# Second MLP of a two-layer hybrid step: the second product of blocks 0 to 2 by seven products of quarters, x kept in DRAM

## The chip, the cores and the metric

The kernel runs on one core of one Trainium2 chip. The metric is the device time of one execution in microseconds, taken as the median of three runs. Engines are named as in the profile: PE (TensorE matmul), PEld (TensorE weight load), DVE (VectorE), ACT (ScalarE), POOL (GpSimd), SP (SyncE, which here only issues DMAs).

## The reference: what is computed

One inference step of a trunk of two layers over 128 context tokens and 512 latent tokens, width 1024. Layer 0 mixes tokens by pooling, layer 1 by bidirectional retention; each layer then has an MLP of width 4096. Both sub-layers of a layer are gated by a per-channel vector that differs for context and latent tokens:

```
h = rmsnorm(x, norm_mlp_w[i]) * (1 + sc_m) + sh_m
x = x + g_m * (square(relu(h @ w1)) @ w2)
```

All inputs and outputs are f32. After the second MLP one more norm gives the outputs.

## The kernel before

All 640 tokens stay in SBUF transposed: `xall` is [128, 8, 640], eight slices of 128 channels; the tokens are handled in two halves of 320 (`HALF`, index h). Half 0 holds latent tokens alone. In half 1 the last 128 columns are context tokens with a gate of their own, so what is scaled by a gate there takes two instructions (192 and 128 columns, `PARTS`).

**Products.** f32 accuracy comes from operands that are split in a high and a low part (`split`, L142 to 146: ACT casts the high part, L144; DVE subtracts it from the source, L145). A product of two split operands is three matmuls (`mm3`, L205 to 207), each 128x128 weights times 128x320 activations. Weights come by SP as pieces of 1 MB (`load`), and are split when they are next needed.

**The MLP** (`mlp`, from L747) goes over four blocks of 1024 hidden channels. In each block the first product (w1) gives the hidden tiles, each passed through relu and square on ACT (L851, L852) and split into the operands `a` of the second product; the second product (w2) is `gemm`, eight output slices by two halves, 24 matmuls each, and DVE adds each result times the gate to x (`add_to_x`, L500).

In blocks 1 to 3 (`FAST`) the first product is made by **seven products of quarters** in place of eight: `quarters` (L767) makes sums and differences of the four quarters of h once (48 DVE instructions of 320 columns: L776 to 783 and the splits); `seven` (L790) makes the weight sums (L802 to 806, 128x1024 each) and splits; `fast` (L812) runs the seven products p = 0 to 6, 12 matmuls for each of two slices t, twice per block (half 0 and 1 of the block's channels), and combines the results on ACT and DVE (L832 to 842). In block 0 the first product is ordinary: slices 0 to 3 in `follow`, right behind the norm, slices 4 to 7 by `gemm`. Before, the instructions of `quarters` stand between those of block 0's second product.

**What sets the order.** Each engine runs its own list in order; the lists come from the order of the program text and a scheduler at build time, so an instruction waits behind all that stand ahead of it on its engine. Seven tiles `t` (`th()`, L131) serve as scratch for all of this. In the second MLP (the last stage of the kernel, before the last norm) i is 1.

Of the kernel before, what the change touches and what calls it, by code (L numbers as in the profile page):

```python
# [27 lines left out]
DV = 512  # L28
# [35 lines left out]

STEPS = (((0, 0, 0, 0, 3, 2, 3, 0), (0, 1, 0, 1, 0, 0, 0, 0)),
# [45 lines left out]
def hybrid_kernel(ctx: ExitStack, tc: tile.TileContext, x_prompt, x_sample, state_ret, c, c_ctx, w_ada, b_ada,  # L111
# [15 lines left out]
    tmp = ctx.enter_context(tc.tile_pool(name="tmp", bufs=1))  # L127
    psum = ctx.enter_context(tc.tile_pool(name="psum", bufs=8, space=PSUM))


    def bank():  # L131
        return psum.tile([128, 512], F32, tag="ps", name=nm("ps"))

# [4 lines left out]
    def t5():  # L138

        return tmp.tile([128, 512], F32, tag="t", name=nm("t"), bufs=7)  # L140
# [68 lines left out]
    def gemm(ws, act, h, mid=None):  # L209


        out = [bank()[:, 0:HALF] for _ in ws]
        for k in range(len(act)):
            if mid and k == len(act) // 2:
                mid()
            for o, w in zip(out, ws):
                mm3(o, [z[:, k] for z in w], [z[:, HALVES[h]] for z in act[k]], k == 0, k == len(act) - 1)
        return out
# [8 lines left out]
    tab_sb = const.tile([128, C_N], F32, name="tab_sb")  # L227
    nc.scalar.dma_start(out=tab_sb[:, 0:C_ROPE], in_=tab[:, 0:C_ROPE])
    ident = tab_sb[:, C_ID:C_ID + 128]
    ones_d = const.tile([128, 128], F32, name="ones_d")  # L230
    V.memset(ones_d, 1.0 / D)
    ones_v = const.tile([128, 128], F32, name="ones_v")
    V.memset(ones_v, 1.0 / DV)
# [184 lines left out]
    xall = xp.tile([128, KD, TOK], F32, name="xall")  # L418
# [132 lines left out]
    with tc.tile_pool(name="pool", bufs=1) as pp:  # L551
        extra[:] = [(wst, 2), (pp, 3), (pp, 3), (wst, 2), (pp, 3)]
# [89 lines left out]
        def load_tables():  # L642
            nc.sync.dma_start(out=win_sb, in_=win)
            nc.sync.dma_start(out=tab_sb[:, C_ROPE:], in_=tab[:, C_ROPE:])
# [61 lines left out]
    def decays():  # L706
# [25 lines left out]

        npos = const.tile([128, 896], I16, name="npos")
        G.iota(npos, [[1, 896]], base=-384, channel_multiplier=-1)
        ipos = const.tile([128, 2, 512], I16, name="ipos")
        G.iota(ipos[:, 0, :], [[1, 512]], base=1, channel_multiplier=0)
        G.iota(ipos[:, 1, :], [[-1, 512]], base=512, channel_multiplier=0)
# [7 lines left out]
        tables.extend((lg, nlg, npos, ipos, zeta))  # L745
# [3 lines left out]
    def mlp(i, sq, norm, hm, step, along):  # L749

        with tc.tile_pool(name=f"hid{i}", bufs=1) as hid:

# [7 lines left out]
            def get(b, n):  # L760

                for o in range(1, AHEAD + 1):
                    if b * 8 + n + o < 64 and not ((b * 8 + n + o) // 16 in FAST[i] and (b * 8 + n + o) // 8 % 2 == 0):
                        gets[(b * 8 + n + o) // 8]((n + o) % 8)
                return gets[b](n)
# [79 lines left out]

            for b in range(4):
                act = [[hid.tile([128, TOK], F32R, tag=f"a{n}{e}", name=nm("a")) for e in "hl"] for n in range(8)]

                def hidden(n, h, ps):
                    r, f = th(), th()  # L850
                    S.activation(r, ps, AF.Relu)  # L851
                    S.activation(f, r, AF.Square)  # L852
                    split(f, *[z[:, HALVES[h]] for z in act[n]])
# [9 lines left out]
                if b in FAST[i]:  # L863
                    if b == FAST[i][0]:
# [6 lines left out]
                    get(2 * b + 1, 0)  # L871
                else:
                    for n in range(4 if b == 0 else 0, 8):
                        if n == FREE:
                            room[0] = room[1]
                        for h in range(2):
                            hidden(n, h, gemm([get(2 * b, n)], hm, h)[0])
                        step(STEPS[b][0][n])
                if i == 0 and b == 0:
                    step(until=(0, 5))  # L880
                if b == 3:
                    room[:] = [None, None]
                    return tail(lambda n, h: gemm([get(7, n)], act, h)[0], mod[i][5], along)
                for n in range(KD):
# [22 lines left out]
    with tc.tile_pool(name="ret", bufs=1) as rp:  # L907
        def r5():
            return rp.tile([128, 512], F32R, tag="r5", name=nm("r5"), bufs=6)

        lg, nlg, npos, ipos, zeta = tables
# [5 lines left out]
        def queries_keys(hd):  # L917
# [10 lines left out]
            def take(nmq, t, h, ps):  # L928
                ct = C_ROPE if nmq == "q" else C_ROPE + 144
# [11 lines left out]
                if t == 0:  # L941
                    cb, sb = (tab_sb[:, ct + o:ct + o + 8][:, rw].unsqueeze(2).to_broadcast(shape) for o in (0, 8))
                else:
                    cb, sb = (tab_sb[:, ct + o:ct + o + 64].unsqueeze(1).to_broadcast(shape) for o in (16, 80))
# [301 lines left out]
```

## Time and profile before

| | |
|---|---|
| median of three runs | 1621.87 us (1620.45 to 1624.13) |
| profiled execution, its own time | 1622.77 us |
| span of its core in the trace | 1621.0 us |
| mean granted TensorE clock | 0.994 |
| PE busy in the span | 1582.8 us (98%) |
| DVE, ACT, POOL busy | 1164.0, 727.0, 11.7 us |
| start of the second MLP on PE | 1166.07 us |

A line of the profile names the source line, the engine, the operation and out<-in by the names of the program's tiles, then the shape; a recorded duration is longer than the distance between two starts, since instructions of one engine overlap a little, so where work is back to back the distance of the starts is the cost.

### The profile page before, as it was taken

What the parts mean: (1) busy time and instruction counts of PE and PEld (TensorE: products, weight loads), DVE (VectorE), ACT (ScalarE), POOL (GpSimd) and SP (SyncE); (2) the same over time, 40 slices, a digit from 0 to 9 for tenths busy, and PEclk for the clock granted to TensorE, in tenths of its full rate; (3) what the DMA queues carried; (4) which work ended last, traced back from release to release, by engine and by line L of the source; (5) the groups of instructions that cost most, each with busy time, mean ns of one, the idle gap of its engine ahead of it and who ended that gap; (6) DMA issues with size and microseconds to landing.
All of it is one profiled execution on the core that took longest, in us unless ns stands there. A gap on an engine that the chain in (4) does not pass through costs nothing. (4 is left out here: it accounts for less than half of the span.)

```text
span 1621.0 us, 24493 instructions
## 1 busy us (share of the span) xinstructions
PE 1582.8 (98%) x9897; PEld 1473.6 (91%) x9897; DVE 1164.0 (72%) x2254; ACT 727.0 (45%) x1338; POOL 11.7 (1%) x26
## 2 busy tenths in 40 slices
PE   6999999999999999999999999999999999999997
PEld 3459999999999988889889988998899999999997
DVE  6879996676766687886797678778967573554654
ACT  6747326336156354433442443353464371451640
POOL 0000000000000000000000000000000000000000
PEclk9999999999999999999999999999999999999999
DMA  9744333333314123323304241322032132131221
GB/s 356 252 141 146 105 105 104 104 124 111 105 53 156 45 70 128 96 79 130 128 29 156 63 146 64 118 92 91 26 105 79 34 124 78 53 104 53 95 75 66
DMA packets 137954, 169.83 MB, mean 105 GB/s; under 512 B 3512, under 2 KB 111472, under 8 KB 137840
## 3 DMA queue, kind: packets, MB, share of 16 engines
q1 hardware_dynamic: 134800, 161.28, 30.2%
q0 software_dynamic: 1312, 4.20, 0.8%
q10 hardware_dynamic: 1728, 2.78, 0.5%
q8 instruction: 78, 1.28, 0.3%
q14 instruction: 36, 0.29, 0.1%
HBM read 161.43 MB, written 6.82 MB: 104 GB/s over the span
## 5 line engine op out<-in xcount | busy, mean ns | idle before, releaser
L144 ACT CAST whi<-wst 128x1024 fp32r<-128x1024 f32 x245 | 254.4, 1049 | 422.5 <-PE ps L206 200.8
L145 DVE TENSOR_TENSOR wlo<-wst,whi 128x1024 fp32r<-128x1024 f32 x245 | 297.3, 1223 | 136.5 <-ACT whi L144 124.0
L205 PE MATMUL ps<-a,whi 128*128 128x320 f32 x896 | 277.2, 310 | 1.2 <-ACT a L144 1.2
L206 PE MATMUL ps<-a,whi 128*128 128x320 f32 x896 | 277.3, 310 | 0.1
L207 PE MATMUL ps<-a,wlo 128*128 128x320 f32 x896 | 276.2, 309 | 0.0
L500 DVE SCALAR_TENSOR_TENSOR xall<-ps,mod,xall 128x320 f32<-128x320 f32 (+2 forms) x288 | 115.7, 436 | 151.6 <-PE ps L207 150.4
L206 PEld LDWEIGHTS ps<-a,whi 128*128 128x128 f32 x896 | 168.2, 188 | 2.1 <-DVE a L145 1.7
L205 PEld LDWEIGHTS ps<-a,whi 128*128 128x128 f32 x896 | 167.9, 188 | 1.8 <-ACT a L144 1.7
L207 PEld LDWEIGHTS ps<-a,wlo 128*128 128x128 f32 x896 | 168.0, 188 | 0.0
L389 DVE SCALAR_TENSOR_TENSOR acc<-wst,c,acc 128x256 f32<-128x256 f32 x336 | 137.6, 483 | 0.0
L205 PE MATMUL ps<-tq,whi 128*128 128x320 f32 x288 | 89.0, 309 | 0.0
L206 PE MATMUL ps<-tq,whi 128*128 128x320 f32 x288 | 89.0, 309 | 0.0
L207 PE MATMUL ps<-tq,wlo 128*128 128x320 f32 x288 | 89.0, 309 | 0.0
L206 PE MATMUL ps<-A,whi 128*128 128x320 f32 x256 | 78.9, 309 | 0.0
L205 PE MATMUL ps<-A,whi 128*128 128x320 f32 x256 | 78.9, 312 | 0.0
L207 PE MATMUL ps<-A,wlo 128*128 128x320 f32 x256 | 78.2, 309 | 0.0
L145 DVE TENSOR_TENSOR a<-t,a 128x320 fp32r<-128x320 f32 x128 | 61.8, 488 | 22.7 <-ACT a L144 22.2
L435 ACT ACTIVATE t<-xall 128x320 f32<-128x320 f32 x56 | 26.0, 471 | 81.2 <-DVE xall L500 81.2
L852 ACT ACTIVATE t<-t 128x320 f32<-128x320 f32 x128 | 60.5, 473 | 1.8
L144 ACT CAST a<-t 128x320 fp32r<-128x320 f32 x128 | 58.5, 457 | 1.5
L207 PEld LDWEIGHTS ps<-tq,wlo 128*128 128x128 f32 x288 | 54.1, 188 | 0.0
L205 PEld LDWEIGHTS ps<-tq,whi 128*128 128x128 f32 x288 | 54.1, 188 | 0.0
(406 smaller groups left out, 4004.4 us busy)
## 6 DMA issues: line engine op xcount, KB each, us to landing
wst<-in_mlp_w_dram SPq DMA_DIRECT2D x64, 1024.0 KB, 5.3
wst<-in_w_ada_dram SPq DMA_DIRECT2D x46, 1024.0 KB, 6.0
wst<-in_ret_w_in_dram SPq DMA_DIRECT2D x24, 1024.0 KB, 5.2
wst<-in_ret_w_out_dram SPq DMA_DIRECT2D x8, 1024.0 KB, 5.0
t<-in_state_ret_dram SPq DMA_DIRECT2D x16, 256.0 KB, 5.5
out_dram<-t POOLq DMA_DIRECT2D x16, 256.0 KB, 2.9
xt<-in_x_sample_dram SPq DMA_DIRECT2D x4, 512.0 KB, 4.8
both<-in_w_ada_dram SPq DMA_DIRECT2D x2, 1024.0 KB, 7.3
```

The source lines that it names most:

```text
L144: S.copy(hi, src)
L145: sub.tensor_tensor(lo, src, hi.bitcast(F32), ALU.subtract)
L205: T.matmul(out, wh, ah, start=first, stop=False, skip_group_check=more)
L206: T.matmul(out, wh, al, start=False, stop=False, skip_group_check=more)
L207: T.matmul(out, wl, ah, start=False, stop=last, skip_group_check=more)
L389: V.scalar_tensor_tensor(acc[j], w[:, k], by, acc[j], ALU.mult, ALU.add)
L435: S.activation(sq[:, o:o + t.shape[-1]], t, AF.Square)
L500: V.scalar_tensor_tensor(x, ps[:, cols], gate[:, d, j:j + 1], x, ALU.mult, ALU.add)
L852: S.activation(f, r, AF.Square)
```

## The change

Nothing of the first MLP, of the mixers and of block 3 of the second MLP is computed in another way. In the second MLP:

- **BOTH.** The second product of blocks 0 to 2 is made by seven products of quarters as well. `hidden_quarters` takes each hidden tile as it comes and makes its operands: for n = 4 to 7 the tile itself, for every quarter differences and sums of hidden tiles (L903, L922 to 931 in the new file), each split in high and low. `fast_to_x` multiplies; each partial result (up to two per output) is scaled by the gate or its negative on ACT (L854) into a `t` tile and added to a DRAM tile `away` by an accumulating DMA that POOL issues (L855): 28 per block, 84 in all, 160 KB each.
- **x in DRAM.** At block 0 SP writes x to `away` by 16 DMAs (L970); before the tail of block 3 SP reads it back by 16 (L999). The space of `xall` holds operand sums meanwhile (`spare`).
- **PART.** In block 0 slices 4 to 7 of the first product are made by `fast`, too (half 1), so `quarters` runs there, between `follow` and `fast`.
- **Room.** The `t` tiles come from a pool of each stage (320 columns in the MLPs); the rope table, two index tables and a constant are made in the retention stage, not at the start.

Instructions before and after, by engine: PE matmuls 168 fewer (24 by PART, 3 x 48 by BOTH), DVE 100 more, ACT 183 more, POOL 84 more, SP 32 more.

```diff
+BOTH = ((), (0, 1, 2))
+PART = (False, True)
...
-            def fast(b, half, ops, take):
-                col = b * 1024 + half * 512
-                ws = seven(mlp_w1[i, :, col:col + 512])
+            def fast(src, half, ops, take):
+                ws = seven(src[:, half * 512:(half + 1) * 512])
...
+            def fast_to_x(src, half, ops):
+                ws = seven(src[:, half * 512:(half + 1) * 512])
+                banks = {}
+                def put(n, h, ps, gate):
+                    t = th()
+                    for j, cols in PARTS[h]:
+                        S.activation(t[:, cols], ps[:, cols], AF.Copy, scale=gate[:, n, j:j + 1])
+                    nc.gpsimd.dma_start(out=away[n][h], in_=t, accum_op=ALU.add)
+                w = next(ws)
+                for p, name in enumerate(("u", "c11", "u", "c21", "u", "u", "c21")):
...
+                        for k in range(4):
+                            mm3(ps, [z[:, k, t * 128:t * 128 + 128] for z in w], ops[p][k], fresh and k == 0, k == 3, not fresh)
+                        n = half * 4 + t
+                        put(*((n, 0), (n, 0), (n + 2, 0), (n + 2, 1), (n + 2, 1), (n, 1), (n + 2, 0))[p], ps,
+                            minus if p in (2, 4) else mod[i][5])
...
+            def hidden_quarters():
...
+                    return ([[a[q + o][h] for q in range(4)] for o, h in ((0, 0), (4, 0))] +
+                            [[sums[q, t] for q in range(4)] for t in range(2)] +
+                            [[a[q + o][h] for q in range(4)] for o, h in ((0, 1), (4, 1))] +
+                            [[sums[q, 2] for q in range(4)]])
...
+                    elif n >= 4:
+                        if h == 1:
+                            t = th()
+                            V.tensor_tensor(t, kept[q], f, ALU.subtract)
+                            split(t, *sums[q, 1])
+                            t = less(t, a[q][0])
+                            split(t, *sums[q, 0])
+                            if (n, 0) in have:
+                                split(less(t, a[n][0], ALU.add), *sums[q, 2])
+                        elif (n, 1) in have:
+                            split(less(f, sums[q, 0], ALU.add), *sums[q, 2])
...
+                    if BOTH[i]:
+                        for n in range(KD):
+                            for h in range(2):
+                                nc.sync.dma_start(out=away[n][h], in_=xT[n][:, HALVES[h]])
+                if b in BOTH[i]:
+                    ops2 = places2()
+                if b in FAST[i] or b == 0 and PART[i]:
+                    if b == (0 if PART[i] else FAST[i][0]):
                         ops = quarters()
-                    for half in range(2):
-                        fast(b, half, ops, hidden)
+                    for half in range(b == 0, 2):
+                        fast(mlp_w1[i, :, blocks[b]], half, ops, hidden)
...
+                if b in BOTH[i]:
+                    for half in range(2):
+                        fast_to_x(mlp_w2[i, blocks[b]], half, ops2)
+                    continue
```

**Two places where the order of instructions changes.** First, DVE at the start of `quarters`. Before, it stands in the second product of block 0 (L776 to 783 and L145 with `tq` or `h0l` are `quarters`; L500 adds a finished result to x; `wlo` is a weight split):

```order
L145 TENSOR_TENSOR wlo_12591<-wst_12531,whi_12590 128x1024
L776 TENSOR_TENSOR t_12953<-h0h_11682,h0l_11683 128x320
L145 TENSOR_TENSOR a_11862<-t_12469,a_11861 128x320
L776 TENSOR_TENSOR t_12955<-h4h_11690,h4l_11691 128x320
L776 TENSOR_TENSOR t_12952<-h0h_11682,h0l_11683 128x320
L500 SCALAR_TENSOR_TENSOR xall<-ps_12478,mod_5_110,xall 128x320
L776 TENSOR_TENSOR t_12954<-h4h_11690,h4l_11691 128x320
L777 TENSOR_TENSOR t_12955<-t_12953,t_12955 128x320
```

In the changed kernel the same instructions stand in block 0's first product. They begin behind an L924 row that subtracts a hidden tile of the last slice of `follow`; from its first L776 on, 44 rows of 320 columns stand there, and then the split of the weights of product p = 2, the last row below:

```order
L779 TENSOR_TENSOR t_12319<-t_12318,t_12319 128x320
L152 TENSOR_TENSOR tq_12276<-t_12321,tq_12276 128x320
L781 TENSOR_TENSOR t_12318<-t_12321,t_12318 128x320
L152 TENSOR_TENSOR h2l_11690<-t_12319,h2h_11689 128x320
L783 TENSOR_TENSOR t_12320<-t_12318,t_12320 128x320
L152 TENSOR_TENSOR tq_12276<-t_12318,tq_12276 128x320
L776 TENSOR_TENSOR t_12341<-h7h_11699,h7l_11700 128x320
L152 TENSOR_TENSOR tq_12276<-t_12320,tq_12276 128x320
L776 TENSOR_TENSOR t_12338<-h3h_11691,h3l_11692 128x320
L776 TENSOR_TENSOR t_12340<-h7h_11699,h7l_11700 128x320
L777 TENSOR_TENSOR t_12341<-t_12339,t_12341 128x320
L152 TENSOR_TENSOR wlo_12403<-wst_12358,whi_12402 128x1024
```

On PE, p = 2 begins 48 matmuls (p = 0 and 1) behind `follow`, and its fifth matmul takes that `wlo`:

```order
L214 MATMUL ps_12426<-h7h_11699,wlo_12367 128x320
L212 MATMUL ps_12370<-tq_12274,whi_12402 128x320
L213 MATMUL ps_12370<-tq_12274,whi_12402 128x320
L212 MATMUL ps_12385<-tq_12274,whi_12402 128x320
L213 MATMUL ps_12385<-tq_12274,whi_12402 128x320
L214 MATMUL ps_12370<-tq_12274,wlo_12403 128x320
```

So `quarters` moved from a stretch where only L500 stood beside it to one where PE's next product reads what it makes.

Second, DVE where block 1 passes from its first product to its second. Before, the end of the first product holds splits alone (`a` is an operand, `wlo` weights):

```order
L145 TENSOR_TENSOR wlo_14682<-wst_14679,whi_14681 128x1024
L145 TENSOR_TENSOR a_14057<-t_14555,a_14056 128x320
L842 TENSOR_TENSOR t_14446<-ps_14466,t_14446 128x320
L145 TENSOR_TENSOR a_14059<-t_14573,a_14058 128x320
L842 TENSOR_TENSOR t_14460<-ps_14481,t_14460 128x320
L145 TENSOR_TENSOR wlo_14739<-wst_14679,whi_14738 128x1024
```

Now sums of hidden tiles (L903 and L931, with their splits) stand there among the weight sums and splits; a part of it:

```order
L152 TENSOR_TENSOR spare<-t_13806,spare 128x320
L903 TENSOR_TENSOR t_13811<-t_13806,a_13226 128x320
L803 TENSOR_TENSOR wst_13864<-wst_13864,wst_13866 128x1024
L903 TENSOR_TENSOR t_13811<-t_13811,a_13227 128x320
L152 TENSOR_TENSOR a_13231<-t_13831,a_13230 128x320
L903 TENSOR_TENSOR t_13835<-t_13831,spare 128x320
L152 TENSOR_TENSOR wlo_13911<-wst_13864,whi_13910 128x1024
L152 TENSOR_TENSOR spare<-t_13811,spare 128x320
L903 TENSOR_TENSOR t_13835<-t_13835,spare 128x320
L152 TENSOR_TENSOR a_13235<-t_13855,a_13234 128x320
```

On PE the operands `a_13231` and `a_13235` are those of product p = 1 of the second product:

```order
L213 MATMUL ps_13914<-a_13231,whi_13872 128x320
L214 MATMUL ps_13914<-a_13230,wlo_13873 128x320
L213 MATMUL ps_13930<-a_13231,whi_13872 128x320
L214 MATMUL ps_13930<-a_13230,wlo_13873 128x320
L212 MATMUL ps_13914<-a_13234,whi_13872 128x320
L212 MATMUL ps_13930<-a_13234,whi_13872 128x320
L213 MATMUL ps_13914<-a_13235,whi_13872 128x320
```

What moved: `a_13231` and `a_13235` are the last two splits of hidden tiles, and in the DVE list they now stand behind most of the block's sums.

## Rows read from the trace of the kernel before

**Rows 1.** The page: busy time by engine, and the chain that ended last.
```profile
PE 1582.8 (98%) x9897; PEld 1473.6 (91%) x9897; DVE 1164.0 (72%) x2254; ACT 727.0 (45%) x1338; POOL 11.7 (1%) x26
...
PE 37%; DVE 2%; DMA 1%; ACT 1%; issue 0%; DVEq 0%; SPq 0%; ACTq 0%
```

**Rows 2.** PE's waits, 1160 to 1621 us: total us, times, longest.
```profile
PE ps L1188 <- DVE sqacc L447: 1.9, 1, 1.9
PE ps L205 <- DVE t L837: 1.4, 1, 1.4
PE ps L205 <- ACT h6h L489: 0.5, 1, 0.5
```

**Rows 3.** PE timeline: start us, duration us; first column gives the distance.
```profile
1195.90 0.31 PE L205 MATMUL ps<-h3h,whi 128*128 128x320 f32 x1
1196.05 0.31 PE L206 MATMUL ps<-h3l,whi 128*128 128x320 f32 x1
1196.19 0.31 PE L207 MATMUL ps<-h3h,wlo 128*128 128x320 f32 x1
1196.34 0.31 PE L205 MATMUL ps<-h3h,whi 128*128 128x320 f32 x1
...
1200.15 0.31 PE L207 MATMUL ps<-h7h,wlo 128*128 128x320 f32 x1
1200.30 0.31 PE L205 MATMUL ps<-h0h,whi 128*128 128x320 f32 x1
```

**Rows 4.** DVE timeline inside `quarters` in block 0's second product.
```profile
1231.14 0.48 DVE L145 TENSOR_TENSOR a<-t,a 128x320 fp32r<-128x320 f32 x1
1231.55 0.49 DVE L776 TENSOR_TENSOR t<-h4h,h4l 128x320 f32<-128x320 f32 x1
1231.95 0.49 DVE L776 TENSOR_TENSOR t<-h0h,h0l 128x320 f32<-128x320 f32 x1
...
1258.21 1.22 DVE L145 TENSOR_TENSOR wlo<-wst,whi 128x1024 fp32r<-128x1024 f32 x1
1259.35 0.48 DVE L145 TENSOR_TENSOR tq<-t,tq 128x320 fp32r<-128x320 f32 x1
```

**Rows 5.** DVE, lines by form, 1160 to 1621 us: busy, mean ns, idle before.
```profile
L145 DVE TENSOR_TENSOR wlo<-wst,whi 128x1024 fp32r<-128x1024 f32 x78 | 95.5, 1224 | 61.9 <-ACT whi L144 52.5 <-PE ps L207 9.3
L500 DVE SCALAR_TENSOR_TENSOR xall<-ps,mod,xall 128x192 f32<-128x192 f32 x37 | 15.4, 418 | 71.5 <-PE ps L207 71.5
```

**Rows 6.** ACT timeline: relu, square and a weight cast at the end of `follow`.
```profile
1200.71 0.43 ACT L851 ACTIVATE t<-ps 128x320 f32<-128x320 f32 x1
1201.03 0.46 ACT L144 CAST a<-t 128x320 fp32r<-128x320 f32 x1
1201.38 0.48 ACT L852 ACTIVATE t<-t 128x320 f32<-128x320 f32 x1
1201.75 0.43 ACT L851 ACTIVATE t<-ps 128x320 f32<-128x320 f32 x1
...
1202.79 1.05 ACT L144 CAST whi<-wst 128x1024 fp32r<-128x1024 f32 x1
1203.73 0.47 ACT L144 CAST a<-t 128x320 fp32r<-128x320 f32 x1
```

**Rows 7.** Stretches of the norm: us, busy PE, PEld, DVE, ACT, POOL, granted PE clock.
```profile
1171.00:1175.00 4.00, 2.83 (x8) 1.61 (x8) 4.00 (x10) 1.60 (x3) 0.00 (x0) 0.75 0.00 0
1175.00:1176.40 1.40, 1.40 (x7) 1.40 (x7) 1.40 (x3) 0.00 (x0) 0.00 (x0) 0.50 0.35 80
1176.40:1200.00 23.60, 23.60 (x162) 23.60 (x162) 16.49 (x32) 16.72 (x42) 0.00 (x0) 1.00 0.28 88
```

**Rows 8.** PE timeline in the second of these stretches.
```profile
1175.30 0.47 PE L206 MATMUL ps<-h0l,whi 128*128 128x320 f32 x1
1175.56 0.47 PE L205 MATMUL ps<-h0h,whi 128*128 128x320 f32 x1
```

**Rows 9.** DMA issues, KB each, median us to landing; POOL's issue, mean ns.
```profile
wst<-in_mlp_w_dram SPq DMA_DIRECT2D x64, 1024.0 KB, 5.3
...
out_dram<-t POOLq DMA_DIRECT2D x16, 256.0 KB, 2.9
...
L1021 POOL DMA_DIRECT2D out_dram<-t x16 | 8.7, 547 | 1074.0 <-ACT t L1020 1074.0
```

**Rows 10.** SP timeline: a DMA issued alone; the first ones in the second MLP.
```profile
644.56 0.38 SPq L170 DMA_DIRECT2D wst<-in_ret_w_in_dram  x1
...
1174.68 32.45 SPq L170 DMA_DIRECT2D wst<-in_mlp_w_dram  x4
```

More of the change, by code (lines that the diff above doesn't have):

```diff
@@ L132, in bank @@
         return psum.tile([128, 512], F32, tag="ps", name=nm("ps"))
+    stage = [None, 512]
     def th():
@@ L138, in t5 @@
     def t5():
-        return tmp.tile([128, 512], F32, tag="t", name=nm("t"), bufs=7)
+        return stage[0].tile([128, stage[1]], F32, tag="t", name=nm("t"), bufs=7)
     def split(src, hi, lo, sub=V):
@@ L216, in gemm @@
             for o, w in zip(out, ws):
-                mm3(o, [z[:, k] for z in w], [z[:, HALVES[h]] for z in act[k]], k == 0, k == len(act) - 1)
+                mm3(o, [z[:, k] for z in w], [z[h] if isinstance(z, list) else z[:, HALVES[h]] for z in act[k]], k == 0, k == len(act) - 1)
         return out
@@ L762, in get @@
                 for o in range(1, AHEAD + 1):
-                    if b * 8 + n + o < 64 and not ((b * 8 + n + o) // 16 in FAST[i] and (b * 8 + n + o) // 8 % 2 == 0):
-                        gets[(b * 8 + n + o) // 8]((n + o) % 8)
+                    at = b * 8 + n + o
+                    if at < 64 and at // 16 not in (FAST, BOTH)[at // 8 % 2][i] and not (PART[i] and 4 <= at < 8):
+                        gets[at // 8](at % 8)
                 return gets[b](n)
@@ L844, in fast @@
                     w = after
-            for b in range(4):
[L847 to L853, printed above, removed]
+            def fast_to_x(src, half, ops):
[8 more added lines that the diff above has]
+                for p, name in enumerate(("u", "c11", "u", "c21", "u", "u", "c21")):
+                    after = next(ws, None)
+                    for t in range(2):
+                        fresh = (name, t) not in banks
+                        if fresh:
+                            banks[name, t] = bank()[:, 0:HALF]
+                        ps = banks[name, t]
+                        for k in range(4):
[3 more added lines that the diff above has]
+                            minus if p in (2, 4) else mod[i][5])
+                    w = after
@@ new lines, in mlp, with hidden @@
+            spare = []
+            for b in range(4):
+                if b in BOTH[i]:
+                    hidden, places2 = hidden_quarters()
+                else:
+                    act = [[[hid.tile([128, HALF], F32R, tag=f"a{n}{h}{e}", name=nm("a")) for h in range(2)] for e in "hl"]
+                           for n in range(8)] if BOTH[i] else [
+                        [[z[:, HALVES[h]] for h in range(2)] for z in (hid.tile([128, TOK], F32R, tag=f"a{n}{e}",
+                                                                                name=nm("a")) for e in "hl")]
+                        for n in range(8)]
+                    def hidden(n, h, ps):
+                        r, f = th(), th()
+                        S.activation(r, ps, AF.Relu)
+                        S.activation(f, r, AF.Square)
+                        split(f, *[z[h] for z in act[n]])
@@ L870, in mlp @@
                             next(logs, None)
-                    get(2 * b + 1, 0)
+                    if b not in BOTH[i]:
+                        get(2 * b + 1, 0)
                 else:
@@ L882, in mlp @@
                     room[:] = [None, None]
+                    if BOTH[i]:
+                        back = xp.tile([128, KD, TOK], F32, tag="xall", name="back")
+                        xT[:] = [back[:, d, :] for d in range(KD)]
+                        for n in range(KD):
+                            for h in range(2):
+                                nc.sync.dma_start(out=xT[n][:, HALVES[h]], in_=away[n][h])
                     return tail(lambda n, h: gemm([get(7, n)], act, h)[0], mod[i][5], along)
+                if b in BOTH[i]:
+                    for half in range(2):
+                        fast_to_x(mlp_w2[i, blocks[b]], half, ops2)
+                    continue
                 for n in range(KD):
```

81 lines of the change are left out of this document (62 added, 19 removed).

## The prediction, made before the changed kernel was run

> **What bounds the kernel now.** The page first: PE is busy 98% of the span, and in the chain that ended last nothing else counts [rows 1]. So a matmul that goes is time gained, as long as PE does not wait for it elsewhere. Then PE's waits in the second MLP, which runs from 1166 to 1621 us: the longest is 1.9 us, the next 1.4, the rest half a microsecond each [rows 2]; there is hardly a wait to remove. Then the PE timeline for the price of one matmul: the rows record 0.31 us, but they start 0.15 us apart, three steps in 0.44 us, 0.1467 us each [rows 3]. Last DVE: it is idle for long stretches before L500 and before the weight splits, waiting for PE or for ACT [rows 5], so it has room on average. What matters is whether it has room at the places where the new work stands, since each engine goes through its list in order.
>
> **The gain.** 168 matmuls go: 24 by PART (half 1 of block 0's first product: 168 in place of 192) and 48 in each of three second products (336 in place of 384). At 0.1467 us: 3.5 + 3 x 7.0 = 24.6 us.
>
> **DVE prices.** Back to back, a 320-column instruction starts 0.40 to 0.41 us after the one before, a 1024-column split is followed after 1.14 us [rows 4]. I take 0.405 and 1.14.
>
> **Cost 1: quarters in block 0.** Before, its 48 instructions ran beside a second product that needed none of them, and PE did not wait. Now PE needs them at once. `follow` ends on PE at 1200.3 [rows 3]; p = 0 and 1 (48 matmuls, operands that are there) last 7.04 us, and four matmuls of p = 2 can run on the cast parts, so PE reaches the `wlo` of p = 2 at 1207.9. DVE can begin the 44 rows only behind the L924 of the last slice of `follow`, which needs that slice's relu and square: their like begins at 1200.7 to 1201.8 on ACT, with a cast between them, and ends at about 1202.9 (two relus, a cast of 0.46, a square of 0.48) [rows 6]. From there 44 x 0.405 + 1.14 = 19.0 us: 1221.9. PE stands still for 14.0 us. Next is p = 3: 14 more DVE rows (11 x 0.405 + 3 x 1.14 = 7.9), and between two of them a cast of 1.0 us on ACT [rows 6], 8.9 in all, while PE has 24 matmuls (3.5 us): 5.4 more. Together 19.4 us. Lower bound: if ACT is done at 1201.0 and the p = 3 rows overlap the cast, 16; upper bound: many of these rows depend on a row or on a cast just before them, so with 0.49 us each (the recorded duration, no overlap [rows 4]) 58 rows cost 4.7 more: 24.
>
> **Cost 2: from first to second product, three times.** In blocks 1 and 2 the last slices' results arrive with p = 4 and later of half 1; from the L836 behind p = 4 to the operand `a_13231` stand 34 rows of 320 and 4 of 1024 columns: 34 x 0.405 + 4 x 1.14 = 18.3 us. PE has 98 matmuls until it wants that operand: 14.4 us. With 0.3 us for DVE to start behind PE (a matmul's recorded length [rows 3]): a wait of 4.2. The next operand `a_13235` is 4 rows and one wide one later (2.8 us) against 6 matmuls (0.9): 1.9. Then p = 3 wants a weight sum, a cast and a split that stand behind four more rows and two wide ones: 1.6 + 2.3 + 1.0 + 1.14 = 6.1 against 32 matmuls (4.7): 1.4. That is 7.5 us a block. In block 0 the rows are 35 and 5 (19.9 us) against 99 matmuls (14.5): 5.7 with the start, then 0.7 and 0.8: 7.2. Sum of three: 22.2 us. Lower bound: if the sums stood 4 us earlier than I lay them (ACT's part is not in the rows, but neither is it free), 11; upper bound: rows and ACT's casts alternate, and with 0.49 us each 34 rows cost 2.9 more a block: 31.
>
> **Cost 3: the clock.** Behind the short waits of the norm the granted clock stood at 0.50 of full speed for 1.4 us, 1.2 GHz in place of 2.4 [rows 7], and matmuls began 0.26 to 0.27 us apart [rows 8]: five at 0.12 us more, 0.6. I take this once for each of four long waits: 2.4 us. The Trainium skill ("TensorE: Matmul & The Clock Gate", What's actually happening) says that the low state is the default and that only activity lifts it, which speaks against a change that makes PE wait; by it each wait would be followed by more slow matmuls than the norm's were. As a mechanism from rows: if the 24 matmuls of one product run at the low level behind each of the four waits, that is 4 x 24 x 0.12 = 11.5 us in place of 2.4.
>
> **Taken at nothing, and under what cover.** ACT: a second product is 336 matmuls, 49 us on PE; ACT has 28 tiles to scale there, the 14 of token half 0 in one instruction and the 14 of half 1 in two, 42 x 0.43 us, as the relu from PSUM [rows 6] = 18 us, and 14 casts of 1.05, 15 us: 33 of 49. If that cover goes, PE waits for a bank. POOL: 84 issues, 0.55 us each in the nearest row [rows 9], one every 1.76 us (12 matmuls). The adding DMA has no row. Nearest is a plain 256 KB store from POOL, 2.9 us to landing [rows 9]; below, nothing at all (its landing is waited for by nobody but the next add to the same tile); above, with twice the traffic on the DRAM side, some 6 us, and I take 3 to 4. Seven `t` tiles at one per 1.76 us allow about 12 us, and two adds to one output are 3.5 us apart, so to 6 us little shows. The Trainium skill ("DMA: Bandwidth & Descriptors", Rules for kernel authors) says that an accumulating DMA reads its destination and writes it later and loses what lands in between, so that the earlier one must have been waited for. That is the wait above, and if the landing were 15 us it would decide (below). SP: 16 writes of x, 0.38 us each [rows 10], stand ahead of the weights of PART's product: 6.1 us. x is final before h is made from it at 1166, and SP's next weight load goes out at 1174.7 [rows 10], so they end in time, within 1 or 2 us. The 16 reads stand behind block 2's last adds and ahead of the weights of block 3's half 1: 3 + 6.1 + 5.3 [rows 9] = 14.4 us against 24.6 of half 0; if that cover goes, some microseconds once. Tables built later: behind 1 us of POOL and one load in the retention stage, nothing up to 2 us.
>
> **The sum.** 1622.8 (the profiled execution's own time) - 24.6 + 19.4 + 22.2 + 2.4 = 1642.2. The median is 0.9 below that execution: **1641.3**.
>
> **The rivals.** *A. DVE keeps up* (the other side). Place: the transitions. If the scheduler's rows fall in time before PE's p = 4 results, because ACT and PE hand over sooner than I laid it out, the 22.2 us vanish, and only quarters is left: 1622.8 - 24.6 + 19.4 + 0.6 - 0.9 = 1617; with that hidden as well 1597. It decides where all waits together are under 24.6 us, or each transition under 1.5. For: DVE is 72% busy, and its idle time [rows 5] is in this very stage. Against: the rows are in order and their counts are fixed; the average doesn't help in a burst. 0.12. *B. Slow adds.* If an add takes 15 us to land, POOL holds two landings one behind the other (p = 0 to 1, p = 3 to 4) in each half of 24.6 us, 30 us and more, so at least 6 us for each of six halves: 36 more, 1677. For: no row shows such a DMA. Against: 2.9 us for a larger plain one. 0.07. *C. The clock stays low* behind each wait: 9 us more, 1650. 0.08. *D. Nothing to see*: gain and waits cancel, with waits of 21 to 28 us: 0.04. That the change does not take the 168 matmuls away is excluded by the count of PE's instructions.
>
> **How the numbers follow.** My forecast, waits of 30 to 55 us and so 1627 to 1652, has 0.69. Slower than before by over 0.2% (3.2 us, about what this measurement can tell from no change): 0.69 + 0.07 + 0.08 = 0.84; same 0.04; faster 0.12. The bounds of the two costs alone give 1622.8 - 24.6 - 0.9 + 16 + 11 + 0.6 = 1625 and 1597.3 + 24 + 31 + 11.5 = 1664. The range takes these and part of A: 1618 to 1666; outside lie the rest of A and B.
>
> **What would show it.** Right: PE waits of 12 us and more at p = 2 of PART's half (waiting for DVE's `wlo`), of 4 to 6 at p = 1 of each second product for an `a` operand from DVE; DVE without idle time in both places; no wait of ACT's L854 for POOL. Cost 1 is wrong if PE's longest wait in block 0 is under 8 us, cost 2 if PE goes from block 1's first to its second product without a wait over 1 us. If L854 waits for POOL, B holds. If PE's waits are as forecast and the clock is 0.50 for long behind them, C does.

## The result, and the profile after

The changed kernel takes 1678.57 us (median of four runs, 1677.13 to 1680.18), the kernel before 1621.16 us beside it: 1.0351 times as long, 95% interval 1.0333 to 1.0369. The direction was forecast, the size was not: 57 us slower, where 20 were expected, and outside the range.

The page after, busy time, granted clock and DMA share by slices, and the queue that POOL feeds:

```profile
PE 1581.0 (94%) x9729; PEld 1466.1 (87%) x9729; DVE 1240.2 (74%) x2354; ACT 807.9 (48%) x1521; POOL 85.3 (5%) x110
...
PEclk9999999999999999999999999999978999989999
DMA  9744323323333233233223313232116618438531
...
q0 software_dynamic: 13408, 17.97, 7.2%
```

Against [rows 1], PE has 168 matmuls less and is busy for hardly less: each lasts longer. In the second MLP (slice 28 on) the clock falls below 9 tenths in three slices, and the DMA engines, at 1 to 4 tenths from slice 3 on, go up to 8.

The stages of the second MLP, each from the first matmul of one to the first of the next, after (us; busy time of PE, PEld, DVE, ACT, POOL; granted clock; DMA share; GB/s):

```profile
1167.75:1202.29 34.54, 31.97 (x196) 29.70 (x195) 27.61 (x57) 22.00 (x52) 0.00 (x0) 0.95 0.25 81
1202.29:1250.68 48.39, 30.25 (x170) 28.95 (x169) 41.88 (x86) 27.23 (x55) 0.00 (x0) 0.75 0.14 44
1250.68:1319.49 68.81, 54.88 (x338) 53.24 (x337) 42.82 (x57) 36.55 (x72) 22.70 (x26) 0.90 0.69 123
1319.49:1369.70 50.21, 49.73 (x338) 49.28 (x337) 37.71 (x57) 35.02 (x69) 1.75 (x2) 1.00 0.32 93
1369.70:1437.31 67.61, 55.99 (x338) 53.91 (x337) 42.47 (x56) 36.27 (x72) 23.45 (x27) 0.90 0.68 125
1437.31:1486.85 49.54, 49.54 (x338) 49.28 (x337) 36.87 (x57) 35.55 (x69) 1.03 (x2) 1.00 0.33 94
1486.85:1554.65 67.80, 56.05 (x339) 54.22 (x338) 42.25 (x55) 36.23 (x71) 23.41 (x27) 0.87 0.68 125
```

and two of them before, the half of block 0's first product that PART changes, and block 0's second product:

```profile
1200.30:1228.46 28.16, 28.16 (x195) 28.16 (x193) 11.37 (x16) 17.10 (x35) 0.00 (x0) 1.00 0.33 108
1228.46:1284.78 56.32, 56.32 (x387) 56.32 (x385) 42.70 (x83) 16.48 (x27) 0.00 (x0) 1.00 0.18 57
```

PART's half went from 28.2 to 48.4 us (+20.2), a second product by quarters from 56.3 to 68.8, 67.6 and 67.8 (+12.5, +11.0 and +11.2; those of blocks 1 and 2 took 56.6 before). The second MLP begins 1.7 us later (1167.75 after 1166.07). Together 56.6 us, where the spans differ by 55.9; the other stages differ by 1.6 at most. At 0.1467 us a matmul, PART's half should last 24.6 us and a second product 49.3. So 23.8, 19.5, 18.3 and 18.5 us too much, 80.1 in all. PE's waits in the trace after, over the second MLP (total, times, longest):

```profile
PE ps L212 <- ACT t L854: 18.5, 3, 7.2
PE ps L212 <- issue: 13.9, 1, 13.9
PE ps L212 <- ACT a L151: 13.4, 5, 6.6
PE ps L214 <- DVE wlo L152: 3.5, 6, 1.3
PE ps L212 <- ACT whi L151: 3.4, 2, 2.5
PE ps L213 <- DVE a L152: 2.6, 2, 1.5
```

and where the largest stand in the PE timeline (start, duration, and in brackets the wait ahead):

```profile
1223.40 0.60 PE L212 MATMUL ps<-tq,whi 128*128 128x320 f32 x1 [13.90 <-issue]
1226.08 0.64 PE L214 MATMUL ps<-tq,wlo 128*128 128x320 f32 x1 [1.28 <-DVE wlo L152]
1234.33 0.41 PE L212 MATMUL ps<-tq,whi 128*128 128x320 f32 x1 [2.54 <-ACT whi L151]
1263.44 0.90 PE L212 MATMUL ps<-a,whi 128*128 128x320 f32 x2 [6.60 <-ACT a L151]
1311.00 0.64 PE L212 MATMUL ps<-a,whi 128*128 128x320 f32 x1 [5.31 <-ACT t L854]
1378.16 0.56 PE L212 MATMUL ps<-a,whi 128*128 128x320 f32 x2 [3.01 <-ACT a L151]
1380.18 0.64 PE L213 MATMUL ps<-a,whi 128*128 128x320 f32 x1 [1.47 <-DVE a L152]
1427.46 0.64 PE L212 MATMUL ps<-a,whi 128*128 128x320 f32 x1 [5.93 <-ACT t L854]
1545.85 0.64 PE L212 MATMUL ps<-a,whi 128*128 128x320 f32 x1 [7.22 <-ACT t L854]
```

These waits and the smaller ones in the four stretches are 55 us; the other 25 us of the 80 are matmuls that begin further apart than 0.1467 us, among them some 120 steps of about 0.27 us behind the waits.

**First place: `quarters`.** At 1223.40 PE takes up p = 2, 14 us late. DVE's rows there are back to back at 0.40 us up to the `wlo` that PE waits for next, 1.28 us, up to 1226.08:

```profile
1224.01 0.48 DVE L776 TENSOR_TENSOR t<-h7h,h7l 128x320 f32<-128x320 f32 x1
1224.41 0.48 DVE L777 TENSOR_TENSOR t<-t,t 128x320 f32<-128x320 f32 x1
1224.82 1.21 DVE L152 TENSOR_TENSOR wlo<-wst,whi 128x1024 fp32r<-128x1024 f32 x1
```

"Issue" at 1223.40 means that the profile names no releaser for the wait of 13.9 us. ACT's timeline shows what ended then:

```profile
1222.51 0.46 ACT L151 CAST tq<-t 128x320 fp32r<-128x320 f32 x1 [0.34 <-DVE t L783]
1222.88 0.74 ACT L831 COPY t<-ps 128x320 f32<-128x320 f32 x2
```

p = 2 adds to the bank of p = 0, so PE can't begin it before L831 has copied p = 0's result out. L831 stands in ACT's list behind twelve casts of `quarters`, each of which waits for DVE's sums. The first of the two copies ends at 1223.30 and PE begins 0.10 us later; the same 0.10 us stand between them in e2 and e8. The operands of p = 2's first matmuls were ready by 1214. So what held PE first was a bank that ACT emptied late, and only then `wlo`. Without L831 PE would have run four matmuls and stood until 1226 all the same.

**Second place: the end of each second product.** ACT's timeline in block 2:

```profile
1544.17 1.04 ACT L151 CAST whi<-wst 128x1024 fp32r<-128x1024 f32 x1 [8.30 <-DMA wst<-in_mlp_w_dram]
1545.12 0.67 ACT L854 ACTIVATE t<-ps,minus 128x192 f32<-128x192 f32 x2
```

ACT stands 8.30 us at the cast of weights for the *next* stage, whose load has not landed. SP had issued it at 1532.21, 12 us before; in the kernel before such a load took 5.3 us [rows 9]. Behind it in ACT's list is L854, which could run, and PE's p = 5 adds to the bank that L854 reads: PE waits 7.22 us, up to 1545.85. The same stands in block 0 at 1309.33 (6.39 us) and in block 1 at 1425.78 (7.01 us). Before, DVE emptied the banks (L500), and each `gemm` took a fresh one.

**What the DMAs cost.** The changed kernel's POOL group (mean ns of an issue):

```profile
L855 POOL DMA_DIRECT2D away<-t x84 | 73.4, 1019 | 394.6 <-ACT t L854 344.8 <-DMA away<-t 39.6 <-ACT whi L151 6.1
```

and the page's DMA issues (KB each, median us to landing):

```profile
away<-t POOLq DMA_DIRECT2D x84, 160.0 KB, 4.3
```

Issue takes 1.02 us, about twice that of the plain store of 256 KB [rows 9], and the landing 4.3 us where the larger store took 2.9.

### The profile page after: what moved, and what is told of

The parts are those of the page before. It is cut to its first block, busy times and chain, and to the rows that moved or that the text cites. A ratio compares the mean times of both kernels' runs of the same rounds, so it can differ in the third digit from the quotient of the medians.

```text
span 1676.9 us, 24802 instructions
## 1 busy us (share of the span) xinstructions
PE 1581.0 (94%) x9729; PEld 1466.1 (87%) x9729; DVE 1240.2 (74%) x2354; ACT 807.9 (48%) x1521; POOL 85.3 (5%) x110
## 5 line engine op out<-in xcount | busy, mean ns | idle before, releaser
L152 DVE TENSOR_TENSOR wlo<-wst,whi 128x1024 fp32r<-128x1024 f32 x266 | 321.2, 1220 | 180.3 <-ACT whi L151 177.1
L151 ACT CAST whi<-wst 128x1024 fp32r<-128x1024 f32 x266 | 274.8, 1046 | 360.3 <-DMA wst<-in_mlp_w_dram 111.0
L212 PE MATMUL ps<-a,whi 128*128 128x320 f32 x704 | 223.0, 319 | 33.9 <-ACT t L854 18.5
L213 PE MATMUL ps<-a,whi 128*128 128x320 f32 x704 | 223.0, 317 | 2.7 <-DVE a L152 2.6
L214 PE MATMUL ps<-a,wlo 128*128 128x320 f32 x704 | 221.7, 315 | 1.4 <-DVE wlo L152 1.4
L212 PEld LDWEIGHTS ps<-a,whi 128*128 128x128 f32 x704 | 135.0, 193 | 37.1 <-ACT t L854 19.2
L213 PEld LDWEIGHTS ps<-a,whi 128*128 128x128 f32 x704 | 136.1, 193 | 5.4 <-DVE a L152 5.2
L214 PEld LDWEIGHTS ps<-a,wlo 128*128 128x128 f32 x704 | 136.0, 193 | 2.2 <-DVE wlo L152 2.2
L504 DVE SCALAR_TENSOR_TENSOR xall<-ps,mod,xall 128x192 f32<-128x192 f32 (+2 forms) x192 | 76.2, 433 | 59.3 <-PE ps L214 58.6
L212 PE MATMUL ps<-tq,whi 128*128 128x320 f32 x312 | 98.3, 316 | 16.4 <-issue 13.9
L213 PE MATMUL ps<-tq,whi 128*128 128x320 f32 x312 | 98.0, 315 | 0.0
L855 POOL DMA_DIRECT2D away<-t x84 | 73.4, 1019 | 394.6 <-ACT t L854 344.8
L212 PEld LDWEIGHTS ps<-tq,whi 128*128 128x128 f32 x312 | 60.2, 193 | 17.1 <-issue 14.1
L213 PEld LDWEIGHTS ps<-tq,whi 128*128 128x128 f32 x312 | 60.2, 193 | 0.0
```

Source lines behind the costliest of these rows:

```text
L151: S.copy(hi, src)
L152: sub.tensor_tensor(lo, src, hi.bitcast(F32), ALU.subtract)
L212: T.matmul(out, wh, ah, start=first, stop=False, skip_group_check=more)
L213: T.matmul(out, wh, al, start=False, stop=False, skip_group_check=more)
L214: T.matmul(out, wl, ah, start=False, stop=last, skip_group_check=more)
L504: V.scalar_tensor_tensor(x, ps[:, cols], gate[:, d, j:j + 1], x, ALU.mult, ALU.add)
```

## The experiments

Theory 1: DVE and ACT lists with bursts of new rows make PE wait where it reads their results at once. Theory A: the adding DMAs are dear in themselves and make weights and L854 late. Rivals stand in the expectations. Each edit is against the changed kernel unless another is named. The kernel before took 1621.8 to 1623.9 us beside these runs.

**e1: PART undone.**

```diff
-PART = (False, True)
+PART = (False, False)
```

> Only PART is undone: block 0's first product is ordinary again, quarters runs beside block 0's second product. Theory 1 (PE waits for DVE where quarters is wanted at once; the wait also costs slow matmuls behind it): the 13.9 us wait at p = 2 and the 4 us behind it go, with some 4 us of slow matmuls, 24 matmuls (3.5 us) come back, and block 0's passage to its second product gets shorter since its last hidden tiles come spread out: 1678.6 - 20 - 3 = about 1655. Theory 2 (the adding DMAs and what they hold up are the whole matter): 1678.6 + 3.5 = 1682, or no gain beyond 3 us.

1664.25 us (1.0256, 1.0223 to 1.0290): 14 less, not 23. The waits at PART's p = 2 and 3 are gone, but on DVE `quarters` now ran from 1290 to 1310 us: not beside block 0's second product (1232 to 1283 us) but behind it, in block 1's first, with PE's wait for L831 there. The 8.5 us for weights stand in block 1's second product. PE's waits over the second MLP, part:

```profile
PE ps L212 <- ACT t L854: 12.0, 6, 6.1
PE ps L212 <- ACT t L831: 10.5, 1, 10.5
PE ps L212 <- ACT whi L151: 9.7, 3, 8.5
```

**e2: BOTH undone, PART kept.** `BOTH = ((), ())`.

> Only BOTH is undone: second products are ordinary, x stays in SBUF, no adding DMA; PART stays. Theory 1: against the kernel before 24 matmuls less (-3.5 us), and quarters still stands between follow and fast, so a wait of 13 to 19 us at p = 2 and 3 with 3 to 5 us of slow matmuls: 1621 + 14 to 20 = 1635 to 1641. Theory 2: 1617 to 1619.

1643.24 us (1.0127, 1.0093 to 1.0161), 2 above theory 1's range. The wait is where it was, and behind it 1.28 us for `wlo` and 1.80 for the weights of p = 3 are all that is left of it:

```profile
PE ps L212 <- issue: 13.5, 1, 13.5
```

**e3: both undone.**

> PART and BOTH undone: what is left of the change is where tiles and tables lie (scratch tiles by stage, tables built in the retention stage). Theory 1 and 2: like the kernel before within 0.2%, or up to 1.7 us more, which is by how much the changed kernel reaches the second MLP later. Rival: 4 us or more, if the later tables hold up the retention stage.

1626.91 us (1.0025, 1.0010 to 1.0041). The later tables cost some 3 us by these runs (interval 1.6 to 6.7), 1.7 by the start of the second MLP in the changed kernel: a wait of 2.7 us for DVE at the start of the retention stage that the kernel before has not. So e3 to e2, PART alone: +16.3 us. From e2 to the changed kernel, BOTH: +35.3.

**e4: plain stores.** On e1, the DMAs store in place of adding, and the sum of the partial results is left out:

```diff
-                    nc.gpsimd.dma_start(out=away[n][h], in_=t, accum_op=ALU.add)
+                    nc.gpsimd.dma_start(out=away[n][h], in_=t)
```

> As e1, and the 84 DMAs to DRAM store and do not add (the sum over partial results and blocks is left out). Same number, bytes, issues and order of DMAs, same waits between two DMAs on one tile. Theory A (the adding is dear on the DMA engines, 160 KB take them as long as 400 KB of a plain load; weights land late, ACT waits for them ahead of L854, PE waits for L854): L854 waits of PE go from 5 to 7 us a block to under 2, the DMA share in the second products from 0.8 to about 0.5; 12 to 20 us less than e1. Theory B (POOL's issues and its waits for the earlier DMA on the same tile hold L854): within 5 us of e1.

1643.15 us (1.0126, 1.0093 to 1.0159): 21.1 less than e1. Its POOL group:

```profile
L855 POOL DMA_DIRECT2D away<-t x84 | 45.4, 542 | 383.5 <-ACT t L854 363.6 <-DMA away<-t 14.6 <-ACT whi L151 2.6
```

The landing took 2.2 us (4.8 in e1). The POOL queue from 1250 to 1640 us, packets, MB and share of the DMA engines:

```profile
q0 software_dynamic: 3744, 12.78, 9.1%
```

and the same queue and stretch of e1:

```profile
q0 software_dynamic: 11470, 13.05, 24.8%
```

Nearly the same bytes in a third of the packets, at 9.1% in place of 24.8% of the engines: byte for byte an adding DMA took 2.7 times as long as a plain one (24.8 / 13.05 against 9.1 / 12.78). PE's waits for L854 went from 12.0 to 0.8 us, all its waits between 1200 and 1620 us from 44.2 to 27.6, ACT's for weight loads from 26.6 to 12.3. The 8.5 us for weights in block 1's second product stayed (8.8), so they don't come from the adding. Theory A's wait goes as it says, but B could have a part in it, since the landing halved too; e12 tests this.

**e5: `quarters` between the halves of block 0's second product.** On e1: `ops = quarters()` moved behind `fast_to_x` of half 0.

> As e1 (PART undone), and quarters is called between the two halves of block 0's second product, not before block 1. In e1 it came so late that PE waited 10.5 us for L831 (behind casts of quarters on ACT) and 4 us for tq operands in block 1, with slow matmuls behind. Theory 1 (a burst of DVE rows costs only where PE's next product reads it): these 14 us and some 2 us of slow matmuls go: 1664 - 14 to 17 = 1647 to 1650. Theory 2 (scratch tiles held by the adding DMAs delay quarters wherever it stands): 1658 or more.

1659.78 us (1.0224, 1.0171 to 1.0277). 4.5 less, with 5.6 us between its own two runs, and not 14. The time is theory 2's, but the waits in block 1 are gone, and a new one of 12.5 us stands in half 1:

```profile
1279.56 0.63 PE L212 MATMUL ps<-spare,whi 128*128 128x320 f32 x1 [12.54 <-ACT t L854]
```

ACT's casts of `quarters`, each waiting for a DVE row, stand ahead of L854. So a burst beside a second product by quarters is not free even where no product reads it: it holds ACT, which empties PE's banks.

**e6: merged adds.** On e5, two partial results of one output are summed by DVE before the DMA:

```diff
+                if (n, h) in open_sums:
+                    t = open_sums.pop((n, h))
+                    for j, cols in PARTS[h]:
+                        V.scalar_tensor_tensor(t[:, cols], ps[:, cols], gate[:, n, j:j + 1], t[:, cols],
+                                               ALU.mult, ALU.add)
+                    nc.gpsimd.dma_start(out=away[n][h], in_=t, accum_op=ALU.add)
+                    return
...
```

> As e5, and the two partial results of one output are added by DVE into one scratch tile before the DMA: 16 adding DMAs a block, not 28 (48 in all, not 84), for 12 DVE instructions or pairs a block (6 us of DVE a block). Theory A (the adding on the DMA engines is what makes weights late and holds L854): 36 of 84 DMAs less, so 36/84 of the 21 us that plain stores saved against e1, 9 us, and a little more since few waits for a full queue are left: 9 to 15 us less than e5. Theory B (DVE is the bound in the second product as well): no gain, or slower.

1651.62 us (1.0174, 1.0133 to 1.0214): 8.2 less than e5, just under A's range of 9 to 15.

**e7: late sums.** On e6, the sums for p = 6 are made behind p = 1 of the second product.

> As e6, and the sums that only p = 6 of the second product reads (4 a block) are made behind p = 1 of the second product, not in the passage from first to second product: 14 DVE rows leave the 38 to 40 rows there, 16 come later. Theory 1 (the passage waits because PE's p = 1 stands behind all DVE rows of the block): the waits for an a operand in blocks 1 and 2 (2.7 and 1.5 us) and the slow matmuls behind go: 3 to 5 us a block, 6 to 12 us in all. Rival (they wait for the last hidden tiles' own relu, square and split, on ACT and DVE, which come as late as before): under 3 us.

1657.36 us (1.0209, 1.0172 to 1.0246): 5.7 more than e6. In blocks 1 and 2 the waits for `a` operands fell to 1 us, as theory 1 says, and PE waits for weights two products on, 5.50 and 6.29 us; in block 0 it waits 14.7 us for them. Together:

```profile
PE ps L212 <- ACT whi L151: 26.5, 3, 14.7
```

against 6.4 us in e6.

**e8: PE kept busy in the long wait.** In PART's half, behind p = 1 (`fill` is 92 there, 0 elsewhere):

```diff
+                    if fill and p == 1:
+                        idle = bank()[:, 0:HALF]
+                        for r in range(fill):
+                            T.matmul(idle, w[0][:, r % 4, 0:128], ops[1][r % 4][0], start=r == 0, stop=r == fill - 1)
```

> The changed kernel (PART and BOTH on) with 92 more matmuls that nobody reads, between p = 1 and p = 2 of PART's half, where PE waits 13.9 us: 92 x 0.1467 = 13.5 us. If the clock falls because PE waits: the granted clock stays at full speed up to p = 2, the 22 slow matmuls of this stretch go to under 10, 2 to 5 us less than the changed kernel's 1678.6, so 1674 to 1677. If the slow steps come from something else (the weights' or operands' arrival): 1678 to 1680.

1677.05 us (1674.31 to 1679.80; 1.0330, 1.0277 to 1.0384): no gain that these runs can tell. The clock, by stretches of e8:

```profile
1210.00:1223.00 13.00, 13.00 (x91) 13.00 (x90) 13.00 (x34) 4.61 (x10) 0.00 (x0) 1.00 0.01 2
1223.00:1226.00 3.00, 3.00 (x22) 3.00 (x22) 3.00 (x9) 1.48 (x4) 0.00 (x0) 1.00 0.00 0
1226.00:1234.00 8.00, 5.73 (x27) 5.17 (x25) 8.00 (x18) 4.86 (x13) 0.00 (x0) 0.79 0.00 0
```

and of the changed kernel:

```profile
1210.00:1223.00 13.00, 0.00 (x0) 0.00 (x0) 13.00 (x34) 5.53 (x13) 0.00 (x0) 0.56 0.00 1
1223.00:1226.00 3.00, 1.41 (x4) 1.03 (x4) 3.00 (x7) 1.08 (x3) 0.00 (x0) 0.50 0.00 0
1226.00:1234.00 8.00, 5.70 (x20) 5.30 (x20) 6.80 (x14) 5.32 (x12) 0.00 (x0) 0.62 0.00 0
```

In e8's trace everything stands 3.3 us later from the start of the second MLP on, so p = 2 begins at 1226.79. With PE busy the clock stays at 1.00 (2.4 GHz) up to p = 2, without it it is 0.50 (1.2 GHz) there. But behind the next wait it fell all the same: PART's half has 33 slow steps, the changed kernel's 32, not under 10 as expected, and the half is no shorter (49.1 us against 48.4). The next waits grew, for `wlo` from 1.28 to 1.84 us and for the weights of p = 3 from 2.54 to 3.32: here DVE sets the pace, and a slow PE costs little more. So in this stretch the slow steps lie partly under DVE's time.

**e9: the next stage's casts behind L854.** On e5, with an order on ACT's list (`tc.issue_after`) that puts the casts of the next p = 0 and 1 behind the L854 of p = 5.

> As e5, and one order on ACT: the weight casts of the next stage's p = 0 and 1 are issued behind the L854 of p = 5 (no wait is added, only the place in ACT's list). Theory C (the adding DMAs make a weight load late, ACT stands at its cast, and L854, which has what it needs, stands behind it; PE waits for L854 because p = 5 adds to the same bank): the L854 waits at the end of the second half (4.6, 3.7 and 3.4 us) go, with some 1 us of slow matmuls each; up to 3 us a block come back as a wait for the cast at the next stage: 3 to 12 us less than e5. Theory B (scratch tiles and POOL's queue hold L854): the waits stay, within 2 us of e5.

1664.93 us (1.0261, 1.0231 to 1.0292): 5 more than e5, as much as e5's own two runs lie apart; neither theory's time. PE's L854 waits at the ends are gone; in their place it waits for weights (`wlo` 16.0 us in nine waits, `whi` 22.2 in three). The order also held back the casts of half 1, which was more than meant, so the test is not clean. What it shows is that this order gave nothing back.

**e10: blocks 1 and 2 only.** On e6: `BOTH = ((), (1, 2))`, x written to DRAM at block 1, `quarters` in block 0's ordinary second product.

> As e6 (merged adds, PART undone), but only blocks 1 and 2 have the second product by quarters; quarters stands in block 0's ordinary second product as in the kernel before. Theory 1 (a burst of DVE and ACT work costs where PE's banks are read by engines that hold it, and nothing beside L500): block 0 costs nothing, blocks 1 and 2 keep 7.0 us of gain each and pay what they pay in e6, 6 to 8 us of waits and 3 of slow matmuls: 1622 + 2 (tables) + 2 x 2 to 4 = 1628 to 1634, that is 18 to 24 us less than e6. Theory 2 (every block pays alike): a third of e6's excess of 28 goes, 1642.

1633.78 us (1.0078, 1.0056 to 1.0101), 17.8 less than e6, as theory 1 forecast: of all versions with a second product by quarters the nearest to the kernel before, and slower still. PE's waits in block 1:

```profile
1344.63 0.56 PE L212 MATMUL ps<-a,whi 128*128 128x320 f32 x2 [3.08 <-ACT a L151]
1346.65 0.64 PE L213 MATMUL ps<-a,whi 128*128 128x320 f32 x1 [1.46 <-DVE a L152]
1356.97 0.42 PE L212 MATMUL ps<-spare,whi 128*128 128x320 f32 x1 [1.55 <-ACT whi L151]
```

Six us of waits and the slow matmuls behind them eat the 7.0 us gain: from the first matmul of block 1 to that of block 2 110.2 us pass, 106.3 before.

**e11: p = 1 last.** On e10, the second product runs its seven in the order 0, 2, 3, 4, 5, 6, 1; p = 0 and 1 have DMAs of their own; e9's order on ACT.

> As e10, and p = 1 of the second product comes last (its operands, the block's last hidden tiles, come last); p = 0 and 1 are added by DMAs of their own (20 a block, not 16), the others merged; ACT's casts for the next stage behind L854 as in e9. Theory 1 (the passage waits for operands of p = 1): the 2.7 to 3.0 + 1.5 us waits of blocks 1 and 2 go, PE next waits for p = 2, whose sums come 5 to 7 us before the last hidden tiles: a wait of 0 to 4 us in place of 4.4, and less slow clock: 3 to 8 us less than e10, 1622 to 1630. Theory 2 (the passage is bound by DVE's rows altogether, whichever product is asked first): within 3 us of e10.

1637.77 us (1.0094, 1.0062 to 1.0126): 4 more than e10, where theory 1 had 3 to 8 less and theory 2 within 3. The `a` waits are gone, and p = 2 waits for its bank instead:

```profile
1352.54 0.63 PE L212 MATMUL ps<-spare,whi 128*128 128x320 f32 x1 [9.88 <-ACT t L872]
```

L872 (L854's like) stands on ACT behind the casts of the hidden sums. Whichever product was asked first waited, so it is not p = 1's place alone that costs; the passage holds more DVE and ACT rows than PE has matmuls to cover them. (The other two edits, more DMAs and e9's order, may have a part in the 4 us.)

**e12: a second target for the second add.** On e1, with the later of two adds of a half to another DRAM tile (the sum of the two left out).

```diff
-                    nc.gpsimd.dma_start(out=away[n][h], in_=t, accum_op=ALU.add)
+                    first = (n, h) not in begun
+                    begun.add((n, h))
+                    nc.gpsimd.dma_start(out=away[n][h] if first else other[n][h], in_=t, accum_op=ALU.add)
```

> As e1, and the second add to one output within a half goes to a second DRAM tile (also set to x at block 0, 16 more SP writes; the sum of the two is left out), so POOL never waits for a landing 3.5 us after the issue; bytes, adds and issues stay. Theory A (the adding DMAs are dear in themselves: 1.1 us of POOL each, 2.7 times a plain store's time on the DMA engines): POOL's waits for DMA go from 37 us to under 8, the L854 waits of PE stay above 8 us in all, and the time is within 4 us of e1's 1664. Theory B (the wait of one add for the one before is what costs, so the landing time decides): 10 us less or more, 1654 or under, most of the 21 us that plain stores gained.

1665.33 us (1.0258, 1.0229 to 1.0288): 1 more than e1. POOL no longer waits for a landing; its waits in e12:

```profile
POOL away L859 <- ACT t L856: 331.0, 31, 148.4
POOL other L859 <- ACT t L856: 45.5, 22, 6.9
```

against e1's

```profile
POOL away L855 <- DMA away<-t: 36.9, 11, 8.1
```

37 us of POOL's waits vanish and nothing is gained, and PE still waits 13.9 us for L856 (L854's like): theory B falls. Nor do the scratch tiles hold L854: in the changed kernel, e1, e4 and e12 every wait of over 0.5 us of this line at a semaphore ends 0.04 us behind the end of a matmul of PE (20, 18, 29 and 23 waits), so it waited for PE and not for a landing. The 21 us of e4 are the adding itself; the weight loads that come late beside it are the way to PE that the traces show.

## Why the prediction was wrong in size

**What held.** The gain: 168 matmuls at 0.1467 us (at full clock, block 2's first product lasts 49.54 us for 336). Cost 1, 19.4 us forecast: waits of 13.9 + 1.28 + 2.54 + 0.41 = 18.1, at the place named; p = 2 had 15.2 (14.0 forecast), p = 3 3.0 (5.4). One step in it was wrong, without harm to the time: it let four matmuls of p = 2 run before PE stands at DVE's `wlo`, but PE stood 13.9 us ahead of the first of them, for the bank that ACT's L831 had to copy; `wlo` came last, so the whole was right. PART alone gave +16.3 (e3 to e2), where -3.5 + 19.4 + 0.6 = 16.5 was forecast, in part by luck: the waits in e2 are 16.6 us, less than forecast, and the slow matmuls more. Cost 2, 22.2 us: 6.60 + 0.45 + 0.87 + 0.69 in block 0, 5.4 in block 1, 4.4 in block 2, 18.4 in all. The upper bound was not needed there. Here, too, PE waited first for ACT, the cast of the `a` operand (6.60, 3.01 and 2.71 us), and then for DVE's split of it (1.47 and 1.13 in blocks 1 and 2); the prediction had DVE alone.

**What failed, first: "taken at nothing" for the adding DMA.** The step said that up to 6 us of landing little would show, since two adds to an output are 3.5 us apart and seven tiles allow 12 us. The landing was inside that in the median, 4.3 us (20 of the 84 took over 6, the longest 9.8), and the waits between adds cost nothing (e12). What I left out is that the DMA has a price besides its landing: 24.8% of the DMA engines' time in place of 9.1%, and 1.0 to 1.2 us on POOL in place of 0.5. Stores in place of adds gave 21.1 us (e4). In the changed kernel, where plain stores were not tried, L854's 18.5 us in three waits are where late weights show. The Trainium skill ("DMA: Bandwidth & Descriptors", Rules for kernel authors) says to wait for the earlier DMA before adding to the same bytes. That wait did not decide: e12 leaves none that the profile shows, and the time stays. What of the 21 us is the late weights and what the issue on POOL is not separated.

**Second: ACT's cover.** I counted 33 of 49 us of work and called it cover. ACT was busy for 36.2 to 36.6 of 68 us, near what I counted. But it goes in order, and with L831 and L854 it stands on PE's path; one late weight load ahead of L854 (8.30 us) or one burst of casts (13.9 us at p = 2, 12.5 in e5, 9.9 in e11) went straight through. The average hid what the list does, the very argument that I made for DVE.

**Third: cost 3.** 2.4 us for four long waits; the rows give about 25 us of steps over 0.1467 us, some 14 of it in about 120 steps at the low level. Behind the 13.9 us wait the clock stood at 0.50, and low stretches followed shorter waits too, 3.01 and 1.47 us in block 1. Rival C had the mechanism and at 11.5 us less than half the size. That the clock falls because PE waits is shown by e8 for the longest wait: 1.00 with PE busy, 0.50 without. By how much the time would fall without the 25 us is not shown, since e8's gain lay within its spread and its slow steps were no fewer. The Trainium skill ("TensorE: Matmul & The Clock Gate", What's actually happening) says that the low state is the default and that activity lifts it. The trace agrees, with the 1.00 and 0.50 of e8.

**The rivals.** B's 1677 is the measured time, by accident: its mechanism, landings of 15 us one behind the other, fell with 4.3 us and with e12, and its sign, L854 waiting for POOL, did not come. A fell: the waits alone were 55 us, against the 24.6 from which it decides.

The sum in its place, in us: -24.6 + 18.1 (cost 1) + 18.4 (cost 2) + 18.5 (L854) + 25 (slow matmuls) + 1.7 (tables) = 57.1, where the spans differ by 55.9. This adds up one trace; it does not show what each term would give back alone. By runs, PART is +16.3, BOTH +35.3 and the rest of the change some 3.

## What to carry to other kernels

When an engine with slack takes over emptying PE's banks, it is on the critical path from then on: read its list for every instruction ahead of that one which can wait for a DMA or another engine, and don't count its average busy time as cover. Price a new kind of DMA by engine time and issue as well as by landing, and if no row has it, hold the estimate open to several times the plain one. Fewer matmuls are worth their full time only where operands for them come no later; the burst of sums between two products, 18 us of DVE here against 14 of PE, must fit before the next product, and moving sums (e5, e7) or asking for another product first (e11) only changed which product waited.

## What the runs showed of the hardware that was not expected

- An adding DMA of 160 KB went in packets of 1.1 KB (13.05 MB in 11470) where the plain store had 3.4 KB (12.78 MB in 3744), took 2.7 times the DMA engines' time byte for byte, 1.0 to 1.2 us to issue where the store took 0.54, and landed in 4.3 to 4.8 us (medians), where the store took 2.2.
- Whether two adds wait for one another made no difference to the time (e12: 1 us, inside the runs' spread), though POOL stood 37 us less.
- The clock fell to 1.2 GHz behind waits of 3.01 and 1.47 us (block 1, 0.50 from 1380.0 to 1383.5 us), and in e8 behind one of 1.84 us, and stayed there for ten matmuls and more; with PE kept busy through the place of the 13.9 us wait it stayed at 2.4 GHz.
- PE's longest wait, 13.9 us, has no releaser in the profile; the timelines of three runs (the changed kernel, e2, e8) put its end 0.10 us behind the end of ACT's copy out of the bank.
